# SSD heads, B-by-C and y products: full-height operands and another order of the products

## The chip, the cores and the metric

The kernel runs on one core of a Trainium2 chip, in one launch. The metric is device time in microseconds (us) of that core, the median of several runs. TensorE does the matrix products, VectorE and ScalarE the elementwise work and the emptying of PSUM, GpSimd a few copies and sums; SyncE issues all loads and stores.

## The reference

One layer of a hybrid decoder on 304 token columns: 16 meta tokens, 256 prompt tokens, and 8 running sequences of 4 tokens each. Model width is 2048, everything in fp32.

- `proj = rmsnorm(x) @ w_in`; its columns go to an RG-LRU group and to a Mamba-2 SSD group (z, xs, B, C, dt).
- SSD: 32 heads of 64 features in 4 groups; each group has one B and one C of 128 states. The tokens go in chunks of 128. With `acum` the running sum of `dt*A` inside a chunk:

```
lmat   = exp(acum_i - acum_j) * dt_j          (j <= i, per head)
y_diag = ((C_i . B_j) * lmat) @ xs_j          (inside a chunk)
states = sum_j B_j xs_j exp(acum_end - acum_j) dt_j ;  h = decay * h + states
y_off  = (C_i . h_start) * exp(acum_i)        (from the chunks before)
y      = y_diag + y_off + d_skip * xs ;  then gated by silu(z), normed, projected
```

- After it `x + mix @ w_out`, an MLP `relu(x @ w_up)^2 @ w_down`, and a last norm. The states of both groups are outputs too.

## The kernel before

Everything is kept with features on the partitions and the 288 or 304 tokens along the free axis. Each dense layer is a row of blocks: a block takes 16 k-slices of a 2048x128 piece of weights. The weights arrive in fp32 (1 MB a block, `prep`, L78) and are split into a high part (`whi`, ScalarE) and a low part (`wlo`, VectorE), so that a block is 48 products in fp32r (`gemm`, L101: high by high, high by low, low by high). A block uses two halves of 8 slices; `whi` and `wlo` have four buffers each, which is two blocks.

The SSD work has no stretch of its own. It is a generator, `ssd_core(g)`, one for each of the 4 groups, and `pump()` advances it by one step after every fourth k-slice of a block. So the SSD products lie between the products of the xs and z blocks, from about 143 to 366 us. The program's order is a proposal: the framework's planner, which simulates a timeline (`schedule_with_timeline_sim=True`), puts each engine's instructions in order by readiness and priority, and engines then run in that order.

What matters in `tables` and `ssd_core`:

- `acst` (tables) holds `acum` in two parts: rows 0 to 31 the high part of the 32 heads, rows 32 to 63 the low part. `selr` is a matrix of zeros and ones that picks a head's two rows. Both have 64 rows. The columns of `acum` itself come from weights tiled four times, so its rows 64 to 127 hold copies.
- `head(j)`, for 8 heads a group: one product (L500) of `selr`'s column, broadcast to 128 output rows, with `acst` (288 columns), which puts a head's `acum` on all 128 partitions; then five ScalarE operations read that bank.
- B by C (L471 to L473): two 128x128x128 products in plain fp32 for the prompt chunks, and one for the 32 running tokens, with 32 columns of B as weights, written to 32 partitions. `bd` is a tile with four copies of B's running tokens' 32 columns, made on GpSimd, which L460 has transposed just before.
- `tile_y(t)`, for 4 tiles of 128 features a group: for each chunk c two products of 64 weight columns (L559: one for each head of the tile, written to partitions 0 to 63 and 64 to 127), then one of 128 weight columns (L561, C by the state). `em[c]` is the weighted decay, made by one ScalarE and one VectorE operation a chunk.
- `sample(b)` (L436, L438) treats one running sequence, 8 times a group; its states come and go by DMA.

A plain fp32 product appears in the trace as two records; an fp32r one as one record.

Of the kernel before, what the change touches and what calls it, by code (L numbers as in the profile page):

```python
# [9 lines left out]
F32R = mybir.dt.float32r  # L10
AF = mybir.ActivationFunctionType
# [3 lines left out]
P = 128  # L15
T = 304
M0 = 16
NT = 288
# [11 lines left out]
K_ID, K_MASK, K_SCAN, K_MS, K_ES, K_MB, K_SEL = 0, 128, 256, 560, 592, 720, 728  # L30
# [3 lines left out]
def body(ctx, tc, I, O):  # L34
    nc = tc.nc
    V, A, G, TE, SY = nc.vector, nc.scalar, nc.gpsimd, nc.tensor, nc.sync
# [10 lines left out]
    def nm(s):  # L47
        cnt[0] += 1
        return f"{s}_{cnt[0]}"

    def bigt():
        return big.tile([P, T], F32, tag="big", name=nm("big"))

    def bank():
        return pss.tile([P, 512], F32, tag="s", name=nm("s"))

    def tt(e, out, a, b, op):
        e.tensor_tensor(out, a, b, op=op)  # L58

    def stt(out, a, s, b, op0, op1):  # L60
        V.scalar_tensor_tensor(out, a, s, b, op0=op0, op1=op1)

    def act(out, in_, f, bias=None, scale=None):
        kw = {}
        if bias is not None:
            kw["bias"] = bias
        if scale is not None:
            kw["scale"] = scale
        A.activation(out, in_, f, **kw)  # L69
# [74 lines left out]
    con = cst.tile([P, NCST], F32, name="con")  # L144
# [39 lines left out]
    sp = spa_stack.enter_context(tc.tile_pool(name="spa", bufs=1))  # L184
# [80 lines left out]
    def softplus(out, xin, tmp):  # L265
        ab, r, s, q, acc = tmp
        act(ab, xin, AF.Abs)
        act(ab, ab, AF.Exp, scale=-1.0)
        V.tensor_scalar(r, ab, 2.0, None, op0=ADD)
        V.reciprocal(r, r)  # L270
        tt(V, s, ab, r, MUL)
        tt(V, q, s, s, MUL)
        V.tensor_scalar(acc, q, 1.0 / 17.0, None, op0=MUL)
        for k in (15, 13, 11, 9, 7, 5, 3):
            stt(acc, acc, 1.0 / k, q, ADD, MUL)
        stt(acc, acc, 1.0, s, ADD, MUL)
        V.tensor_scalar(r, xin, 0.0, None, op0=MAX)
        stt(out, acc, 2.0, r, MUL, ADD)
# [44 lines left out]
    def flat(t):  # L323
        return t[:].rearrange("p a b -> p (a b)")

    def dup(e, out, src):
        e.tensor_copy(out[:, 0:3, :], src[:, None, 272:T].to_broadcast([out.shape[0], 3, 32]))
        e.tensor_copy(out[:, 3, :], src[:, 0:32])

    def post_dt(ps):  # L330
        x0 = bigt()
        tt(V, x0[:], ps[:, :T], rsb[:], MUL)
        gens.append(tables(x0))

    def tables(x0):
        b1, b2, b3 = [bigt() for _ in range(3)]
        dt = sp.tile([P, EXT], F32, tag="cv", bufs=2, name="dt")[:, :T]
        th1, th2 = [sp.tile([P, EXT], F32, tag="th", bufs=2, name=nm("th"))[:, :T] for _ in range(2)]
        V.tensor_scalar(x0[:], x0[:], par[:, C_DTB:C_DTB + 1], None, op0=ADD)
        softplus(dt, x0[:], (b1[:], th1, th2, b2[:], b3[:]))  # L340
        nega = cst.tile([P, 1], F32, name="nega")
        act(nega[:], par[:, C_AL:C_AL + 1], AF.Exp)
        V.tensor_scalar(nega[:], nega[:], -1.0, None, op0=MUL)
        dta = x0[:]
        V.tensor_scalar(dta, dt, nega[:], None, op0=MUL)
        acum = b1[:]
        V.tensor_tensor_scan(acum, con[:, K_SCAN:K_SCAN + T], dta, 0.0, op0=MUL, op1=ADD)
        acst = sp.tile([64, NT], F32R, tag="acst", name="acst")
        act(acst[:], acum[0:64, M0:T], AF.Copy)
        tt(V, acst[32:64, :], acum[32:64, M0:T], acst[32:64, :].bitcast(F32), SUB)  # L350
        selr = sp.tile([64, 32], F32R, tag="selr", name="selr")
        act(selr[:], con[0:64, K_SEL:K_SEL + 32], AF.Copy)
        t1 = b2
        V.tensor_copy(t1[0:32, :], dt[0:32, :])
        V.tensor_copy(t1[32:64, :], acum[32:64, :])
        t1d = sp.tile([64, 4, 32], F32, name="t1d")
        dup(V, t1d, t1[0:64])
        yield
        pt = bank()
        ptv = pt[:, 0:192].rearrange("p (c j) -> p c j", j=64)  # L360
        for c, src in enumerate((t1[0:64, 16:144], t1[0:64, 144:272], flat(t1d))):
            TE.transpose(ptv[:, c, :], src, con[0:64, K_ID:K_ID + 64])
        tok = sp.tile([P, 3, 64], F32, name="tok")
        V.tensor_copy(tok[:], ptv)
        yield
        yield
        pl = bank()
        plv = pl[:, 0:96].rearrange("p (c j) -> p c j", j=32)
        for c in (0, 1):
            TE.matmul(plv[:, c, :], con[:, K_ID + 127:K_ID + 128].to_broadcast([P, P]), tok[:, c, 32:64],  # L370
                      start=True, stop=True)
        TE.matmul(plv[:, 2, :], con[:, K_ES:K_ES + P], tok[:, 2, 32:64], start=True, stop=True)
        pd = bank()
        pdv = pd[:, 0:256].rearrange("p (b j) -> p b j", j=32)
        for b in range(8):
            TE.matmul(pdv[:, b, :], con[0:32, K_ID + 4 * b + 3:K_ID + 4 * b + 4].to_broadcast([32, P]),
                      tok[0:32, 2, 32:64], start=True, stop=True)
        we = sp.tile([P, 3, 32], F32, name="we")
        tt(V, we[:], plv, tok[:, :, 32:64], SUB)
        act(we[:], we[:], AF.Exp)  # L380
        decp = sp.tile([P, 2, 32], F32, name="decp")
        act(decp[:], plv[:, 0:2, :], AF.Exp)
        eas = sp.tile([64, 32], F32, name="eas")
        act(eas[:], tok[0:64, 2, 32:64], AF.Exp)
        decs = sp.tile([P, 8, 32], F32, name="decs")
        act(decs[:], pdv, AF.Exp)
        tab.update(tok=tok, we=we, decp=decp, eas=eas, decs=decs, acst=acst, selr=selr)
# [10 lines left out]
    def ssd_core(g):  # L398
        hs = slice(8 * g, 8 * g + 8)
        tok, we, decp, eas, decs, acst, selr = (tab[k] for k in ("tok", "we", "decp", "eas", "decs", "acst", "selr"))  # L400
        B, C = bf[g], cf[g]
        bd = sp.tile([P, 4, 32], F32, tag="dup", bufs=1, name=nm("bd"))
# [67 lines left out]
        pc = bank()  # L470
        TE.matmul(pc[:, 0:128], B[:, 16:144], C[:, 16:144], start=True, stop=True)  # L471
        TE.matmul(pc[:, 128:256], B[:, 144:272], C[:, 144:272], start=True, stop=True)
        TE.matmul(pc[0:32, 256:288], B[:, 272:T], C[:, 272:T], start=True, stop=True)  # L473
        cbm = sq_.tile([P, NT], F32, tag="cbm", name=nm("cbm"))
        tt(V, cbm[:, 0:256].rearrange("p (c j) -> p c j", j=128), pc[:, 0:256].rearrange("p (c j) -> p c j", j=128),
           con[:, None, K_MASK:K_MASK + 128].to_broadcast([P, 2, 128]), MUL)
# [20 lines left out]
        def head(j):  # L497
            h = 8 * g + j
            pbc = bank()
            TE.matmul(pbc[:, 0:NT], selr[:, h:h + 1].to_broadcast([64, P]), acst[:], start=True, stop=True)  # L500
            for c in (0, 1):
                act(em[c][:, j, :], pbc[:, 128 * c:128 * c + 128], AF.Relu, bias=tok[:, c, 32 + h:33 + h], scale=-1.0)
            act(es[:, j, :], pbc[0:32, 256:288], AF.Relu, bias=tok[0:32, 2, 32 + h:33 + h], scale=-1.0)
            q = 64 * (j % 2)
            act(ea[q:q + 64, j // 2, :], pbc[q:q + 64, 0:256], AF.Exp)
# [8 lines left out]

        head(0)
        head(1)
        yield
        sample(0)
# [34 lines left out]
        def tile_y(t):  # L553
            o = 4 * g + t
            py = bank()
            for c in (0, 1):
                for q in (0, 1):
                    j = 2 * t + q
                    TE.matmul(py[64 * q:64 * q + 64, 128 * c:128 * c + 128], xdc[c][:, 64 * j:64 * j + 64],  # L559
                              em[c][:, j, :], start=True, stop=True)  # L560
                TE.matmul(py[:, 256 + 128 * c:384 + 128 * c], hst[c][:, 128 * t:128 * t + 128],  # L561
                          C[:, 16 + 128 * c:144 + 128 * c], start=True, stop=True)
            y = bigt()
            yp = y[:, 0:256]
            tt(V, yp, ea[:, t, :], py[:, 256:512], MUL)
            stt(yp, xf[o][:, M0:272], par[:, C_DSK + o:C_DSK + o + 1], yp, MUL, ADD)
            tt(V, yp, yp, py[:, 0:256], ADD)
            ys_.append(y)

        tile_y(0)  # L570
        yield
        sample(5)
# [30 lines left out]
    def post_x(o):  # L603
        def f(ps):
            xf[o] = bigt()
            post_conv(ps, o, xf[o], rsb if o < 4 else None)
            if o % 4 == 3 and o > 3:
                gens.append(ssd_core(o // 4))
        return f
# [19 lines left out]
    cm = sq_.tile([P, 592], F32R, name="cm")  # L629
    V.tensor_scalar(cm[:], con[:, 0:592], 0.0, None, op0=MUL)  # L630
    gens.append(ssd_core(0))
    run_blocks([(win[8 + o], xa, 0, T, post_x(o)) for o in range(4, 16)], win[24:26])

# [426 lines left out]
```

## Time and profile before

| what | value |
|---|---|
| median of 3 runs | 1643.75 us (1643.62 to 1644.5) |
| the profiled execution | 1644.08 us, of which the span from first to last instruction is 1642.2 us |
| mean granted TensorE clock | 0.995 |
| TensorE busy | 1620.9 us, 99% of the span |
| VectorE busy | 1057.7 us, 64% |
| ScalarE busy | 832.5 us, 51% |

Busy times are unions of records. Records of TensorE overlap (the array works on several products in a pipeline), so the duration of a record is not what a product costs; the distance from one record's start to the next one's is. The form of a TensorE record, as 128*128 or 64*128, is rows of weights by columns of weights.

### The profile page before, as it was taken

Reading aid. Unit: us, or ns where it says so; the run is one execution under the profiler, and the core shown is the slowest. Engines: PE = TensorE matmul, PEld = TensorE weight load, DVE = VectorE, ACT = ScalarE, POOL = GpSimd, SP = SyncE. Lnnn points to the kernel's source line nnn. Section 1 sums busy time; section 2 is a strip of 40 time slices with the busy share of each in tenths; the row PEclk is TensorE's granted clock in tenths of the full one; section 3 lists DMA queues with packets and bytes.
Section 4 is the critical chain, followed back from the end, with each engine's and each line's share of the span. In section 5 each row is a group of like instructions: output and inputs, shape, how many; then the busy total and the mean of one; then the engine's idle time right before and its main releaser. Section 6 shows DMA issues by size and latency. Waiting matters only on the chain.

```text
span 1642.2 us, 28891 instructions
## 1 busy us (share of the span) xinstructions
PE 1620.9 (99%) x11855; PEld 1582.3 (96%) x11855; DVE 1057.7 (64%) x1542; ACT 832.5 (51%) x1299; POOL 243.9 (15%) x311
## 2 busy tenths in 40 slices
PE   7999999999999999999999999999999999999997
PEld 6999888889999999999999999999999999999997
DVE  8998998979887778455565433554444555555554
ACT  5656676557777775344444433443334433344442
POOL 5543323321132321001140000000000000000000
PEclk9999999999999999999999999999999999999999
DMA  6454555544545456544444544545444444544442
GB/s 216 157 178 139 193 183 174 172 176 149 185 140 187 140 182 198 175 169 165 158 172 159 166 168 158 176 154 176 158 166 169 158 176 155 175 158 166 169 158 105
DMA packets 53988, 274.28 MB, mean 167 GB/s; under 512 B 5984, under 2 KB 12768, under 8 KB 24544
## 3 DMA queue, kind: packets, MB, share of 16 engines
q1 hardware_dynamic: 53856, 272.44, 48.7%
q8 instruction: 93, 1.52, 0.4%
q14 instruction: 39, 0.32, 0.1%
HBM read 259.99 MB, written 12.42 MB: 166 GB/s over the span
## 4 chain that ended last, share of the span: by engine, by line
PE 98%; DMA 1%; DVE 0%; SPq 0%; issue 0%; ACT 0%; DVEq 0%
PE g L101 90%; PE s L101 1%; PE s L438 1%; PE s L761 1%; PE s L561 1%; PE s L559 1%; PE s L500 1%; PE s L436 0%; PE s L509 0%; DMA wraw<-in_win 0%; PE s L448 0%; DVE z L58 0%; PE s L520 0%; PE s L586 0%; DMA big<-in_x 0%; SPq L209 0%
## 5 line engine op out<-in xcount | busy, mean ns | idle before, releaser
L58 DVE TENSOR_TENSOR wlo<-wraw,whi 128x1024 fp32r<-128x1024 f32 (+1 forms) x470 | 574.8, 1225 | 427.7 <-ACT whi L69 427.1
L69 ACT ACTIVATE whi<-wraw 128x1024 fp32r<-128x1024 f32 (+1 forms) x470 | 492.2, 1048 | 666.3 <-PE g L101 606.8
L101 PE MATMUL g<-mh,whi 128*128 128x288 f32 x1024 | 303.2, 296 | 0.0
L101 PE MATMUL g<-hh,whi 128*128 128x288 f32 x1024 | 303.0, 296 | 0.0
L101 PE MATMUL g<-hl,whi 128*128 128x288 f32 x1024 | 302.4, 295 | 0.0
L101 PE MATMUL g<-ml,whi 128*128 128x288 f32 x1024 | 302.1, 295 | 0.0
L101 PE MATMUL g<-hh,wlo 128*128 128x288 f32 x1024 | 301.3, 294 | 0.0
L101 PE MATMUL g<-mh,wlo 128*128 128x288 f32 x1024 | 301.1, 294 | 0.0
L101 PE MATMUL g<-xh,whi 128*128 128x288 f32 (+1 forms) x960 | 288.9, 301 | 0.4 <-DVE ext L287 0.4
L101 PE MATMUL g<-xl,whi 128*128 128x288 f32 (+1 forms) x960 | 288.1, 300 | 0.0
L101 PE MATMUL g<-xh,wlo 128*128 128x288 f32 (+1 forms) x960 | 287.9, 300 | 0.0
L101 PEld LDWEIGHTS g<-mh,wlo 128*128 128x128 f32 x1024 | 192.9, 188 | 0.0
L101 PEld LDWEIGHTS g<-hh,wlo 128*128 128x128 f32 x1024 | 192.8, 188 | 0.0
L101 PEld LDWEIGHTS g<-hh,whi 128*128 128x128 f32 x1024 | 192.5, 188 | 0.0
L101 PEld LDWEIGHTS g<-hl,whi 128*128 128x128 f32 x1024 | 192.5, 188 | 0.0
L101 PEld LDWEIGHTS g<-ml,whi 128*128 128x128 f32 x1024 | 192.3, 188 | 0.0
L101 PEld LDWEIGHTS g<-mh,whi 128*128 128x128 f32 x1024 | 191.9, 187 | 0.0
L101 PEld LDWEIGHTS g<-xh,whi 128*128 128x128 f32 x960 | 180.7, 188 | 4.6 <-issue 1.8
L101 PEld LDWEIGHTS g<-xh,wlo 128*128 128x128 f32 x960 | 181.0, 189 | 3.1 <-issue 0.5
L101 PEld LDWEIGHTS g<-xl,whi 128*128 128x128 f32 x960 | 180.8, 188 | 3.4 <-issue 0.7
L101 PE MATMUL g<-lh,whi 128*128 128x288 f32 x256 | 75.7, 296 | 0.0
L101 PE MATMUL g<-sh,whi 128*128 128x288 f32 x256 | 75.7, 296 | 0.0
(273 smaller groups left out, 2323.1 us busy)
## 6 DMA issues: line engine op xcount, KB each, us to landing
wraw<-in_win SPq DMA_DIRECT2D x69, 1024.0 KB, 5.0
wraw<-in_wup SPq DMA_DIRECT2D x64, 1024.0 KB, 4.9
wraw<-in_wdn SPq DMA_DIRECT2D x64, 1024.0 KB, 4.9
wraw<-in_wout SPq DMA_DIRECT2D x32, 1024.0 KB, 5.0
h<-in_stssd SPq DMA_DIRECT2D x32, 256.0 KB, 3.0
out_sssd<-h SPq DMA_DIRECT2D x32, 256.0 KB, 3.2
wraw<-in_win SPq DMA_DIRECT2D x12, 256.0 KB, 6.5
big<-in_x SPq DMA_DIRECT2D x16, 152.0 KB, 3.7
```

The lines of the kernel that those rows point to most:

```text
L58: e.tensor_tensor(out, a, b, op=op)
L69: A.activation(out, in_, f, **kw)
L101: TE.matmul(o, a[:, k % 8, :], b[:, c0:c1], start=n == 0, stop=n == 3 * NK - 1)
L438: TE.matmul(po[0:66, :], cm[:, 66 * b:66 * b + 66], a[:], start=b == 0 and n == 0, stop=b == 7 and n == 1)
L500: TE.matmul(pbc[:, 0:NT], selr[:, h:h + 1].to_broadcast([64, P]), acst[:], start=True, stop=True)
L559: TE.matmul(py[64 * q:64 * q + 64, 128 * c:128 * c + 128], xdc[c][:, 64 * j:64 * j + 64], em[c][:, j, :], start=True, stop=True)
L561: TE.matmul(py[:, 256 + 128 * c:384 + 128 * c], hst[c][:, 128 * t:128 * t + 128], C[:, 16 + 128 * c:144 + 128 * c], start=True, stop=True)
L761: TE.matmul(pr[:, :FL], w_[:, m, :], x_[:], start=n == 0, stop=n == 2)
```

## The change

Three edits, all in the SSD part.

1. `acst` and `selr` get 128 rows in place of 64. Rows 64 to 127 of `selr` are zeros, so the products have the same value; L500 is called with 128 rows.
2. The B-by-C product for the running tokens takes `bd` flattened (128 columns, four copies of the 32) as weights and writes 128 partitions; only the first 32 are read, as before.
3. In `tile_y` the four L559 products of both chunks are issued first, and then the two L561 products.

```diff
-        acst = sp.tile([64, NT], F32R, tag="acst", name="acst")
-        act(acst[:], acum[0:64, M0:T], AF.Copy)
+        acst = sp.tile([P, NT], F32R, tag="acst", name="acst")
+        act(acst[:], acum[:, M0:T], AF.Copy)
         tt(V, acst[32:64, :], acum[32:64, M0:T], acst[32:64, :].bitcast(F32), SUB)
-        selr = sp.tile([64, 32], F32R, tag="selr", name="selr")
-        act(selr[:], con[0:64, K_SEL:K_SEL + 32], AF.Copy)
+        selr = sp.tile([P, 32], F32R, tag="selr", name="selr")
+        act(selr[:], con[:, K_SEL:K_SEL + 32], AF.Copy)
...
-        TE.matmul(pc[0:32, 256:288], B[:, 272:T], C[:, 272:T], start=True, stop=True)
+        TE.matmul(pc[:, 256:288], flat(bd), C[:, 272:T], start=True, stop=True)
...
-            TE.matmul(pbc[:, 0:NT], selr[:, h:h + 1].to_broadcast([64, P]), acst[:], start=True, stop=True)
+            TE.matmul(pbc[:, 0:NT], selr[:, h:h + 1].to_broadcast([P, P]), acst[:], start=True, stop=True)
...
                     TE.matmul(py[64 * q:64 * q + 64, 128 * c:128 * c + 128], xdc[c][:, 64 * j:64 * j + 64],
                               em[c][:, j, :], start=True, stop=True)
+            for c in (0, 1):
                 TE.matmul(py[:, 256 + 128 * c:384 + 128 * c], hst[c][:, 128 * t:128 * t + 128],
                           C[:, 16 + 128 * c:144 + 128 * c], start=True, stop=True)
```

## Rows read from the trace of the kernel before

**Rows 1.** The page: the span, and the chain that ended last by engine.

```profile
span 1642.2 us, 28891 instructions
...
PE 98%; DMA 1%; DVE 0%; SPq 0%; issue 0%; ACT 0%; DVEq 0%
```

**Rows 2.** The SSD stretch: us, busy us by engine (instructions), clock, DMA.

```profile
143.00:366.00 223.00, 223.00 (x1492) 189.07 (x1492) 195.46 (x324) 140.29 (x316) 76.59 (x92) 0.99 0.51 175
```

**Rows 3.** Waits of TensorE's weight loads, 143 to 366: us, times, longest us.

```profile
PEld s L500 <- issue: 7.4, 26, 0.8
...
PEld s L561 <- issue: 5.5, 32, 0.2
```

**Rows 4.** Timeline of TensorE around a single head: start, us, record.

```profile
150.21 0.30 PE L101 MATMUL g<-xh,wlo 128*128 128x304 f32 x1
150.44 0.40 PE L500 MATMUL s<-acst,selr 64*128 64x288 f32 x1
150.77 0.41 PE L101 MATMUL g<-xh,whi 128*128 128x304 f32 x1
151.01 0.30 PE L101 MATMUL g<-xl,whi 128*128 128x304 f32 x1
151.15 0.30 PE L101 MATMUL g<-xh,wlo 128*128 128x304 f32 x1
```

**Rows 5.** Timeline of TensorE at two heads in a row.

```profile
163.76 0.53 PE L500 MATMUL s<-acst,selr 64*128 64x288 f32 x2
164.22 0.44 PE L438 MATMUL s<-h0h,cm 128*66 128x512 f32 x1
```

**Rows 6.** Timeline of TensorE at the y products, first tiles of group 0.

```profile
184.60 0.48 PE L436 MATMUL s<-xr,bm 128*128 128x512 f32 x1
...
185.53 0.44 PE L559 MATMUL s<-em,xdt 128*64 128x128 f32 x4
...
186.45 0.30 PE L101 MATMUL g<-xh,wlo 128*128 128x304 f32 x1
186.68 0.44 PE L559 MATMUL s<-em,xdt 128*64 128x128 f32 x4
187.05 0.49 PE L561 MATMUL s<-cf,hst 128*128 128x128 f32 x2
187.47 0.44 PE L559 MATMUL s<-em,xdt 128*64 128x128 f32 x4
187.84 0.49 PE L561 MATMUL s<-cf,hst 128*128 128x128 f32 x2
```

**Rows 7.** Timeline of TensorE at B by C, group 1.

```profile
200.94 0.39 PE L471 MATMUL s<-cf,bf 128*128 128x128 f32 x2
201.16 0.39 PE L472 MATMUL s<-cf,bf 128*128 128x128 f32 x2
201.48 0.25 PE L473 MATMUL s<-cf,bf 128*32 128x32 f32 x2
201.66 0.41 PE L101 MATMUL g<-xh,wlo 128*128 128x304 f32 x1
201.90 0.30 PE L101 MATMUL g<-xh,whi 128*128 128x304 f32 x1
```

**Rows 8.** Waits of VectorE, 143 to 366: us, times, longest us.

```profile
DVE h L58 <- PE s L436: 8.4, 10, 2.0
DVE wlo L58 <- ACT whi L69: 6.2, 7, 3.5
```

**Rows 9.** Timeline of VectorE: a low part of weights in the z blocks.

```profile
384.70 1.21 DVE L58 TENSOR_TENSOR wlo<-wraw,whi 128x1024 fp32r<-128x1024 f32 x1
```

**Rows 10.** Timeline of TensorE: the first product that reads it.

```profile
388.69 0.30 PE L101 MATMUL g<-xh,wlo 128*128 128x304 f32 x1
```

**Rows 11.** Groups of instructions of VectorE, 143 to 366: busy us, mean ns.

```profile
L58 DVE TENSOR_TENSOR em<-em,cbm 128x1024 f32<-128x1024 f32 x8 | 10.0, 1284 | 0.4 <-ACT em L69 0.3
```

## The prediction

> **What bounds the kernel now.** I read the page first. The chain that ended last is TensorE for 98% of a span of 1642.2 us [rows 1]; so time is gained where TensorE's own row of products becomes shorter, and nowhere else. The span is one profiled execution of 1644.08 us; 1.9 us lie around it, and it stands 0.3 us above the median of 1643.75, from which I subtract.
>
> Next the windows: the SSD stretch is 223 us long, TensorE is busy in all of it, VectorE in 195.46 (88%), ScalarE in 140.29, and the granted clock is 0.99 [rows 2]. Busy here only means that records overlap without a hole. Whether time is lost has to be read from the distances between starts, so I went to the timeline.
>
> There the reader is to see one thing. As long as the form stays 128 rows by more than 64 columns, a fp32r product of 304 columns starts 0.14 us after the one before (151.01 to 151.15 [rows 4]). Where the form changes, three steps in a row are long. Around a single head they are 0.23 (150.21 to 150.44), 0.33 (to 150.77) and 0.24 us (to 151.01) [rows 4]. The waits of the weight loads put those stops down to nothing that the profile knows: "issue", 26 times for the heads and 32 times at L561, 0.2 us each there [rows 3]. TensorE waits for no other engine at these places; it empties itself, and then the first weights of the new form are loaded in plain view. The 32 are two a tile for 16 tiles: each chunk of each tile goes into the 128*64 form and out again.
>
> **The change part by part.**
>
> *Heads.* 24 of the 32 heads stand alone in the timeline as in rows 4, eight stand in four pairs behind L520 as in rows 5. A single one costs 150.21 to 151.01 = 0.80 us for itself and the products on either side. Without a change of form the neighbours take 0.14 each. The head itself I take at 0.13: that is what the second of a pair costs, 0.46 us for two (163.76 to 164.22 [rows 5]) less 0.33 for one [rows 4]. So 0.80 - 0.41 = 0.39 us a head, and 24 x 0.39 = 9.4 us. Its price cannot be far off at 128 rows: a 304-column product of that form takes 0.14 [rows 4], which would take 0.2 us off the sum. A pair: 0.46 - 2 x 0.13 = 0.20, four times 0.8 us. Entering it is not counted, since L520 before it has 16 rows and keeps its own form.
>
> Here a rule can be set beside the row. The row says 0.39 us for one way in and one way out [rows 4]. The Trainium skill ("TensorE: Matmul & The Clock Gate", section "Single matmul latency") gives about 166 ns at full clock as the part of a lone product that a stream of them hides; taken as an estimate for each of two emptyings it would make the heads 24 x 0.33 = 8.0 us in place of 9.4. I keep 9.4, because the row holds the exposed weight load too.
>
> *B by C.* In group 1 the two records of L472 and L473 and the first product behind take 201.16 to 201.90 = 0.74 us [rows 7]. Afterwards L473 has 128 weight columns, so its two records cost what L471's two do, 200.94 to 201.16 = 0.22 [rows 7], though only 32 columns stream. 0.22 + 0.22 + 0.14 = 0.58, a gain of 0.16, times 4 groups 0.6 us. The lower bound is nothing (if four times the weights eat it). No new wait: `bd` is read by L460 shortly before, and the tile that shares its buffer is made at the end of the group.
>
> *y products.* In tiles 1 to 3 of each group the two chunks stand back to back or nearly so: 187.05 to 187.84 = 0.79 us is one L561 and one run of L559 with both changes of form [rows 6]. The new order drops that and adds, without a change of form, four more L559 records (two pairs of 64 columns) behind the first four and two more L561 records behind the first two. The latter are 0.22 as L471's [rows 7]. The former the trace doesn't show, so bounds: a whole run of four is 187.47 to 187.84 = 0.37 with its way out [rows 6], so two pairs are at most 0.37; less the 0.20 that a head's way out costs (0.33 - 0.13 [rows 4, 5]) they are at least 0.17. I take 0.22, since two pairs load as many weight columns as L471's two records, and near the lower end. Gain 0.79 - 0.22 - 0.22 = 0.35 a tile (0.20 to 0.40), for 12 tiles 4.2 us (2.4 to 4.8).
>
> Tile 0 of a group is another matter. Its second chunk starts 185.53, with L436 and more in between (184.60 [rows 6]): the planner had put other work there, because `em[1]` comes one VectorE product, 1.28 us [rows 11], after `em[0]`. It will very likely do so again and pull L561 ahead. Four tiles at 0 to 0.40; I take half of 0.35, 0.7 us in all.
>
> *The rest at nothing.* The copies for `acst` and `selr` happen once, with as many columns as before. ScalarE has 83 us free in the stretch [rows 2] to cover them; uncovered they could cost some tenths. No DMA is added or moved. VectorE's and ScalarE's work stays the same.
>
> TensorE's row shrinks by 9.4 + 0.8 + 0.6 + 4.2 + 0.7 = 15.7 us; from the bounds 13.2 to 17.2.
>
> *What is late next.* The stretch becomes 223 - 15.7 = 207 us, with 195.46 us of VectorE work in it [rows 2]: 94%. VectorE must therefore close its own waits. The two largest are 8.4 us on L436 and 6.2 us on `whi` [rows 8]; the first is TensorE's doing, the second in part, since `whi` waits for buffers that TensorE frees. If all 14.6 us close, VectorE lags by 15.7 - 14.6 = 1.1 us, less than its reserve where I find it thinnest, in the z blocks: a `wlo` ends at 385.91 [rows 9] and is used at 388.69 [rows 10], 2.8 us later. If only half closes, it lags by 8.4, and 8.4 - 2.8 = 5.6 us are given back. So 0 to 5.6; I take 2.0, nearer to the low end, because waits on a faster engine tend to close and gains come 0.39 us at a time while single waits reach 2.0 us [rows 8].
>
> Net 15.7 - 2.0 = 13.7: 1643.75 - 13.7 = 1630.0 us.
>
> **The rivals.**
>
> *VectorE becomes the bound* and gives back more than 4 us. For: 94% over the stretch. Against: weights are split well ahead inside it. At 5.6 us the time is 1643.75 - 15.7 + 5.6 = 1633.6; to 1638 if 10 are lost.
>
> *The long steps have another cause*, some wait that stays. Then little more than B by C is left, and the time is 1643 to 1644. For: "issue" names no cause. Against: the same step at 32 places of L561, where nothing else is common [rows 3].
>
> *64-row products share the array, and 128 rows lose that.* The Trainium skill ("TensorEngine Tiling", section "Tiling Modes", under "Key Properties") lets tiles work independently, and its "Theoretical Speedup" promises up to twofold for 64 rows. Here two heads in a row would have to cost little more than one; the second costs 0.13 us, as much as its columns need [rows 5]. If the four pairs did lose 0.13 each, 0.5 us: 1630.5.
>
> *Slower: the wait for `em[1]`.* If the planner keeps the written order in tile 0, the third L559 stands at the head of TensorE's queue until `em[1]` is made, and all weight products wait behind it. One VectorE product is 1.28 us [rows 11], four groups 5.1 us, still less than the gain. It decides from 15.7 / 4 = 3.9 us a group, which takes two more VectorE products of that size queued ahead; at 5 us a group the time is 1643.75 - 15.7 + 20 = 1648.
>
> **How the numbers follow.** The forecast has 0.68 (1626.5 to 1633: the 17.2 us bound, and 13.2 less a few given back), VectorE as the bound 0.20, another cause 0.06, shared array 0.02, the wait for `em[1]` 0.04. The range 1625.5 to 1636.5 takes the forecast, the shared array and most of VectorE's case; its upper end is 13.2 - 5.6 = 7.6 us below today, 1636.2. About 0.2% (3.3 us) is what a measurement can tell from no change. Faster by more 0.90, within 0.06, slower 0.04.
>
> **What would show it.** In the profile of the changed kernel L500 has the form 128*128 and its steps to the next product are 0.13 to 0.14 us, with no "issue" wait at it. L559 stands in runs of eight in at least 12 tiles, with about 0.11 us a pair, and the count of waits at L561 falls from 32 to 16 to 20. L473 is 128*128 and takes 0.22. The SSD stretch ends 12 to 16 us sooner, and everything behind keeps its length. I am wrong if TensorE shows new waits on VectorE or ScalarE at L559, L438 or L101 in sum above 4 us, if the z blocks become longer, or if the planner scatters the eight L559.

## The result, and the profile after

| | us |
|---|---|
| before, median | 1643.68 |
| changed kernel, median of 4 runs (1631.34 to 1635.99) | 1633.32, ratio 0.9939 (interval 0.9927 to 0.9951) |
| changed kernel measured again, 4 runs (1631.46 to 1632.72), before 1643.75 | 1631.71, ratio 0.9928 (0.9912 to 0.9945) |
| profiled executions, before and after | 1644.08 and 1631.34 |

The kernel is faster by 10.4 us in one measurement, 12.0 in the other, and 12.7 between the two profiled executions. The forecast was 13.7 us. Both medians lie in the stated range of 1625.5 to 1636.5; the first, 1633.32, lies 0.3 us above the narrower 1626.5 to 1633 of the forecast itself.

The page of the changed kernel, the lines that answer to [rows 1]: the span is 13.0 us shorter, and TensorE's share of the chain that ended last falls from 98% to 92%.

```profile
span 1629.2 us, 28889 instructions
...
PE 92%; DMA 3%; DVE 2%; ACT 1%; issue 1%; POOL 0%; SPq 0%; DVEq 0%; POOLq 0%; ACTq 0%
```

The same 223 us as in [rows 2], of the changed kernel. They now hold work that used to come later (1597 records of TensorE in place of 1492); VectorE's 204.11 us are 92%, and TensorE has 0.9 us without any record.

```profile
143.00:366.00 223.00, 222.10 (x1597) 199.93 (x1597) 204.11 (x347) 147.26 (x328) 89.93 (x97) 1.00 0.55 184
```

Waits of TensorE's weight loads there, against [rows 3]. The nameless stops at the heads fall from 26 to 4. The four that are left, 0.76 us each, stand behind the 16-row product L520, and they were among the 26 before, as long as now. At the second kind of y product (now L562) the stops fall from 32 to 16.

```profile
PEld s L500 <- issue: 3.0, 4, 0.8
...
PEld s L562 <- issue: 2.7, 16, 0.2
```

Timeline of TensorE at a single head, against [rows 4]. The three long steps are gone: 0.14, 0.12, 0.15 us.

```profile
148.31 0.30 PE L101 MATMUL g<-xh,wlo 128*128 128x304 f32 x1
148.45 0.29 PE L500 MATMUL s<-acst,selr 128*128 128x288 f32 x1
148.57 0.31 PE L101 MATMUL g<-xh,whi 128*128 128x304 f32 x1
148.72 0.30 PE L101 MATMUL g<-xl,whi 128*128 128x304 f32 x1
```

A pair of heads, against [rows 5]: 161.35 to 161.72 is 0.37 in place of 0.46. The first of the two heads takes 0.24 us as before, since it still follows L520's other form; the second takes 0.13 in place of 0.22. The product behind takes 0.23 in place of 0.28.

```profile
161.35 0.53 PE L500 MATMUL s<-acst,selr 128*128 128x288 f32 x2
161.72 0.40 PE L438 MATMUL s<-h0h,cm 128*66 128x512 f32 x1
161.95 0.40 PE L438 MATMUL s<-h0l,cm 128*66 128x512 f32 x1
```

The y products of group 0, against [rows 6]: tile 0 stands in two runs of four, at 180.13 and 181.72, with a state's product at 180.50 in between; tile 3 is one run of eight.

```profile
180.13 0.44 PE L559 MATMUL s<-em,xdt 128*64 128x128 f32 x4
180.50 0.50 PE L436 MATMUL s<-xr,bm 128*128 128x512 f32 x1
...
181.72 0.44 PE L559 MATMUL s<-em,xdt 128*64 128x128 f32 x4
...
190.40 0.66 PE L559 MATMUL s<-em,xdt 128*64 128x128 f32 x8
190.99 0.71 PE L562 MATMUL s<-cf,hst 128*128 128x128 f32 x4
191.63 0.46 PE L587 MATMUL s<-xdt,es 32*32 32x64 f32 x5
```

Eight records take 0.59 us (190.40 to 190.99) where four took 0.37 [rows 6], so the four added ones cost 0.22. From its first record to the next form the tile takes 1.23 us. Before, the same tile took 193.96 to 195.53 = 1.57:

```profile
193.96 0.44 PE L559 MATMUL s<-em,xdt 128*64 128x128 f32 x4
...
195.53 0.63 PE L586 MATMUL s<-xdt,es 32*32 32x64 f32 x8
```

B by C in group 1, against [rows 7]. L473 has left L472 and stands 10 us later, behind the transpose of the same `bd`.

```profile
196.84 0.39 PE L472 MATMUL s<-cf,bf 128*128 128x128 f32 x2
196.98 0.39 PE L101 MATMUL g<-xh,whi 128*128 128x304 f32 x1
197.21 0.30 PE L101 MATMUL g<-xl,whi 128*128 128x304 f32 x1
...
206.66 0.27 PE L460 MATMUL s<-con,bd 128*128 128x128 f32 x1
206.77 0.31 PE L473 MATMUL s<-cf,bd 128*128 128x32 f32 x2
206.91 0.39 PE L101 MATMUL g<-xl,whi 128*128 128x304 f32 x1
207.13 0.30 PE L101 MATMUL g<-xh,wlo 128*128 128x304 f32 x1
```

L472 with the product behind it takes 0.37 (before, with L473 between, 0.74), L460 with its followers 206.66 to 207.13 = 0.47 (before 212.41 to 212.67 = 0.26): together 0.84 against 1.00. The lines before:

```profile
212.41 0.27 PE L460 MATMUL s<-con,bd 128*128 128x128 f32 x1
...
212.67 0.30 PE L101 MATMUL g<-xh,whi 128*128 128x304 f32 x1
```

What is new are TensorE's waits on other engines between 143 and 400 us, where the kernel before has none on this list:

```profile
PE s L762 <- ACT xch L69: 0.7, 1, 0.7
PE s L594 <- ACT yo L69: 0.6, 1, 0.6
PE s L438 <- ACT h0h L69: 0.3, 1, 0.3
```

Read from one start to the next, each costs more than its idle time. At the second of them 305.01 to 305.92 is 0.91 us where 0.13 is usual:

```profile
305.01 0.29 PE L101 MATMUL g<-xh,whi 128*128 128x288 f32 x1
305.92 0.47 PE L594 MATMUL s<-con,yo 96*128 96x96 f32 x3 [0.61 <-ACT yo L69]
```

Read so, the three cost 0.90, 0.78 and 0.42, in sum 2.1 us. The last products of the SSD part (L586, now L587) stand 11.3 us sooner, 354.22 in place of 365.52, a little less than the 12 to 16 us of the prediction's sign.

### The profile page after: what moved, and what is told of

It reads as the page before. It is cut to its first block, busy times and chain, and to the rows that moved or that the text cites. A ratio compares the mean times of both kernels' runs of the same rounds, so it can differ in the third digit from the quotient of the medians.

```text
span 1629.2 us, 28889 instructions
## 1 busy us (share of the span) xinstructions
PE 1606.7 (99%) x11855; PEld 1579.8 (97%) x11855; DVE 1058.2 (65%) x1542; ACT 831.3 (51%) x1299; POOL 254.1 (16%) x311
## 4 chain that ended last, share of the span: by engine, by line
PE 92%; DMA 3%; DVE 2%; ACT 1%; issue 1%; POOL 0%; SPq 0%; DVEq 0%; POOLq 0%; ACTq 0%
PE g L101 86%; DMA out_sssd<-h 1%; PE s L101 1%; PE s L762 1%; DMA wraw<-in_win 1%; PE s L438 1%; DMA h<-in_stssd 1%; ACT whi L69 0%; POOL h0l L58 0%; DVE z L58 0%; PE s L562 0%; DVE h L58 0%; PE s L436 0%; PE s L559 0%; PE s L448 0%
```

## The experiments

Theory: what a change of form costs on TensorE is what the change saves, part by part, and what is given back is given back by VectorE, which is nearly full. Rivals: the long steps have another cause; what is given back comes from elsewhere. Each set of runs has its own runs of the kernel before; their medians lie between 1643.5 and 1643.8.

**The three parts alone, and the whole once more.** `heads_only` has the lines of `acst`, `selr` and L500 of the diff, `y_only` the loop in `tile_y`, `bc_only` the B-by-C line; `after_again` is the changed kernel. The edit of `y_only`, against the kernel before, is one line:

```diff
+            for c in (0, 1):
```

> Edit 1 alone: the heads with 128 rows. If the changes of form are what was paid for, 24 single heads give back 0.39 us each and four pairs 0.15 to 0.2 us each: TensorE's row is 10.0 us shorter, the profiled time about 1634 us, and L559 still stands in 32 runs of four. If the long steps had another cause, L500's neighbours keep steps of 0.23, 0.33 and 0.24 us and the time stays within 2 us of before. If VectorE gives back what TensorE saves only once the saving is large, this part alone loses less than 0.5 us to waits.

Measured 1636.42 (1635.12 to 1637.59), 7.3 us less. The stops at L500 are down to 4 and L559 stands in 32 runs of four. TensorE waits for `bd` and for a state's high part:

```profile
PE s L460 <- POOL bd L328: 1.2, 1, 1.2
PE s L438 <- ACT h0h L69: 0.6, 1, 0.6
```

From start to start these two cost 1.4 us (207.91 to 209.46) and 0.8 us (243.14 to 244.07). So of the 10.0 us expected of TensorE's row 7.3 are seen and 2.2 are given back in waits, with this part alone, where less than 0.5 was expected; 0.5 us stays without a place.

> Edit 3 alone: the order of the y products. If the changes of form are paid for, 12 tiles lose one way in and out each, 0.53 us, and pay 0.22 us for the four products that are left: 0.31 to 0.35 us a tile, 3.8 to 4.2 us in all, a time of about 1639.7 us. Tile 0 of each group stays split in two and gives nothing. If what counts is VectorE, which makes em and takes the products away, the time stays within 1 us of before, since its work is the same.

Measured 1640.92 (1638.79 to 1642.80), 2.8 us less; 12 runs of eight and 8 of four, as expected. The time saved is less than the 3.8 to 4.2 us expected; its profile has waits of 0.8 us at L594, 0.4 at L448 and 0.2 at L460, about what is missing.

> Edit 2 alone: 128 columns of weights for the running tokens' B by C. If the form is what is paid for, four places become 0.15 to 0.25 us shorter, 0.6 to 1.0 us in all, which the times can hardly show; the steps in the timeline show it: L472 to L473 0.22 in place of 0.32 us, and the product behind without its extra 0.1. If four times the weights cost four times the load, L473 itself grows from 0.18 to 0.22 us or more and eats a part of that.

Measured 1643.19 (1642.34 to 1644.39), ratio 0.9997 (0.9988 to 1.0007): not told from no change by time. In its timeline L473 is 211.00 to 211.14 = 0.14 us and the product behind takes 0.23 in place of 0.14, so its price is 0.23 with what it does to its neighbour. Its profile has full clock over the SSD part and no wait of TensorE on another engine from 130 to 1600 us.

> The changed kernel once more, for a second profile beside the three parts on one chip. Both theories expect 1631 to 1636 us. If its runs scatter because the granted clock dips to half in some executions and not in others, then the executions with the lower mean clock are the longer ones, about 1.6 us for each 0.001 of the clock; if waits on other engines scatter, time and clock do not go together.

Measured 1631.71. The parts give 7.3 + 2.8 + 0.6 = 10.7 us, the whole 10.4 in the first measurement and 12.0 in this one. So no loss is seen by joining them, as there would be if a full engine gave back the more the larger the saving is. Times and clocks don't go together: 1631.47 and 1631.46 at 0.995 and 0.996, 1632.72 at 0.998.

**96 rows.** The heads' operands cut to 96 rows in place of 128.

```diff
-        acst = sp.tile([P, NT], F32R, tag="acst", name="acst")
+        acst = sp.tile([96, NT], F32R, tag="acst", name="acst")
```

> The changed kernel with 96 rows in place of 128 for the heads' two operands. If what was paid for is the array being set to 64 rows and back, 96 rows do as well as 128: L500's next step 0.13 us, no stop of the weight loads at it, the time 1631 to 1635 us. If the number of rows itself counts, or the sharing of the array by small products, the steps around L500 become long again, up to 0.39 us a head, and the time goes up towards 1641 us.

Measured 1631.72 in one run; no stop is named at L500 but the four behind L520. So the price did not come from having fewer than 128 rows: products of 96 rows stand between those of 128 without a stop, products of 64 rows did not. How the 0.39 us of a 64-row head divide between the emptying of the array and the load of the next weights, no run separates.

**Less work for VectorE.** The kernel leaves out the `d_skip` term of the prompt tokens and the last tap of the convolution for the x columns (`taps` is 3 there).

```diff
-            stt(yp, xf[o][:, M0:272], par[:, C_DSK + o:C_DSK + o + 1], yp, MUL, ADD)
...
-        for k in range(1, 4):
+        for k in range(1, taps):
```

> The changed kernel without some 17 us of VectorE's work in and around the SSD stretch: left out are the d_skip term of the prompt tokens (16 operations of 0.55 us) and the last tap of the convolution of the x columns (16 of 0.5 to 0.66 us in the convolutions that precede the SSD work of their group). If TensorE's new waits of some 2.5 us go back to VectorE being nearly full, they go away: 1629 to 1630 us. If they come from ScalarE's queue, GpSimd or the states' loads and stores, they stay or move: 1631 to 1634 us.

Measured 1634.78 (1634.44 to 1636.67), 1.5 and 3.1 us above the two medians of the changed kernel, though the first of these has a run of 1635.99. From 143 to 366 us VectorE is busy 192.28 us, 12 less than in the changed kernel, and TensorE's waits are

```profile
PE s L438 <- ACT h0h L69: 3.2, 4, 1.2
PE s L438 <- POOL h0l L58: 0.5, 2, 0.3
```

This speaks against the theory of VectorE: with room on VectorE, TensorE waits longer, for the states of the running sequences. It does not rule it out, since the planner orders all engines anew for this kernel.

**Without most of the stores of states.** The kernel leaves out 28 of the 32 stores.

```diff
-            SY.dma_start(O["sssd"][g, :, b, :], h0[:])
+            if b == 0:
+                SY.dma_start(O["sssd"][g, :, b, :], h0[:])
```

> The changed kernel without seven of every eight stores of the running sequences' new states (28 of 32 are left out; only the first sequence of a group is stored). A state's buffer is then free when VectorE has added to it, not when its store has landed, and the next load starts earlier. If TensorE's new waits of the changed kernel (at L438 on the high part h0h or the low part h0l of a state, 0.4 to 1.1 us in each profile) come from the chain store, load, split of a state, they go away and the time is 1629.5 to 1631. If they come from VectorE or ScalarE being full, they stay, and the time is 1631 to 1633.

Measured 1631.42 (1630.43 to 1633.27), not told from the changed kernel. The waits at L438 are gone, as the chain of store, load and split demands, and those at L594 and L762 with them; in their place stands

```profile
PE s L461 <- POOL bd L328: 1.2, 1, 1.2
```

**Five buffers for the states.**

```diff
-                h0 = sq_.tile([P, 512], F32, tag="h0", bufs=4, name=nm("h0"))
+                h0 = sq_.tile([P, 512], F32, tag="h0", bufs=5, name=nm("h0"))
```

> The changed kernel with five buffers for the states in place of four (the space is taken from two of the 24 buffers of the pool called big). Nothing is left out. If the load that waits for the store just before it is what holds up L438, the load now finds a free buffer, the waits at h0h and h0l fall below 0.3 us in sum, and the time is 1629.5 to 1631.5. If the two missing buffers of the other pool are needed, or the waits have another cause, the time is 1631.5 or more.

Measured 1632.79 (1631.49 to 1634.31). The wait at L438 is 0.3 us, and small ones on VectorE add up to 1.2 (L559, L436); no gain. What the two buffers taken from `big` cost was not measured by itself.

**Further places of the same kind.** `em_joint` makes both chunks' decay at once; `best3` adds L520 and L376 at 128 rows; `h5_meta` has these two with five state buffers and separate decays; `meta_dup2` has them with two buffers for `bd`. Of the cuts below the first is that of `em_joint` and `best3`, the second that of `best3`, `h5_meta` and `meta_dup2`, the third that of `meta_dup2`; the rows of L376 and the zeros in L520's weights are not shown.

```diff
-            act(em[c][:], em[c][:], AF.Exp, scale=-1.0)
+        act(em2[:], em2[:], AF.Exp, scale=-1.0)
...
-        TE.matmul(ph[:], bt[96:112, 2, :], xw[96:112, :], start=True, stop=True)
+        TE.matmul(ph[:], bt[:, 2, :], xw[:], start=True, stop=True)
...
-        bd = sp.tile([P, 4, 32], F32, tag="dup", bufs=1, name=nm("bd"))
+        bd = sp.tile([P, 4, 32], F32, tag="dup", bufs=2, name=nm("bd"))
```

> The changed kernel with the weighted decay of both chunks made in one ScalarE and one VectorE operation, so that both chunks of tile 0 are ready at once. The planner then has all eight L559 records of each tile in one run, 16 runs in place of 20. By the price of a way in and out (0.09 before, 0.15 inside the run, 0.10 behind) this gives back four times 0.34 us, 1.4 us: 1630 to 1631 us. If readiness of em was not what split tile 0, or if waiting for the joint product costs more than it saves, the time is not below that of the changed kernel.

Measured 1641.62, scattered from 1634.46 to 1648.03. The 16 runs of eight are there, but TensorE waits more:

```profile
PE s L594 <- ACT yo L69: 2.3, 2, 1.4
PE s L559 <- DVE h L58: 0.7, 2, 0.6
```

That the one long ScalarE operation (1.9 us a group) makes others late is not shown. In front of the first of the two waits at L594 ScalarE itself stood 1.8 us until a state's load had landed, and made `yo` right behind it. The profile is one of the shorter runs; the long ones were not profiled.

> The joint decay, and the same idea in two more places: the product of 16 rows at the start of each group (L520, four times, with 0.09 us in, 1.05 for itself and 0.10 behind) takes 128 rows, with the other rows of its weights set to zero by one more ScalarE operation a group, and the eight products of 32 rows in the tables (L376, once) take 128 rows of the identity and of tok. By the row of L509, which has the same shape with 128 rows (0.46 us), L520 gives 0.78 us a group, 3.1 us; L376 some 0.3; with the joint decay 4.8 us: about 1627 us. If TensorE is no longer what bounds the stretch, because VectorE or the states' loads and stores set the pace, half or less of this is seen: 1629 us or more.

Measured 1639.10 (1631.51 to 1643.58). The profiled execution is the shortest of them and has waits of 1.4 us on VectorE, 1.3 on `h0l` and 0.7 on `h0h`; what the longer ones wait for wasn't profiled.

> The same five buffers, and L520 and L376 with 128 rows as before (3.1 and 0.3 us of TensorE's own row), but with em made in two halves again. If the states' chain was what gave back the gain of the last kernel, the 3.4 us are now seen: 1626.5 to 1628.5, with runs that agree within 2 us. If the gain is given back all the same (VectorE full, joint em innocent), 1631 or more with scattered runs.

Measured 1631.05 (1630.67 to 1632.27), ratio 0.9926 (0.9914 to 0.9938), the lowest median here, though its interval covers the changed kernel's second ratio of 0.9928. My price for L520 was misread. In this kernel the timeline shows

```profile
160.57 1.02 PE L521 MATMUL s<-xw,bt 128*128 128x512 f32 x2
161.03 0.82 PE L501 MATMUL s<-acst,selr 128*128 128x288 f32 x2
161.69 0.39 PE L438 MATMUL s<-h0h,cm 128*66 128x512 f32 x1
```

The two records stand 0.46 us before the next start, but the pair of heads behind them then takes 0.66, where 0.13 a head is usual: part of the long plain fp32 product is paid at its follower. From L520 (L521 here) to L438 it is 1.12 us in place of 1.42 in the changed kernel (160.30 to 161.72). With 0.1 less at the product in front, that is a gain of 0.4 a group, not 0.78. Against these 1.6 us and some 0.3 at L376 stand waits of 1.5 us (`bd` 1.0, `h0h` 0.5).

> The changed kernel with L520 and L376 at 128 rows (3.4 us of TensorE's own row by the rows of L509 and L376), four state buffers as in the changed kernel, and two buffers in place of one for the tile bd shares with the sums at a group's end (one of the 24 buffers of big pays for it), so that GpSimd can make bd early: the wait of L460 on bd was 1.3 us in the last profile. If waits can be taken away one by one, the time is 1628 to 1629.5 us, below the changed kernel. If the stretch is so full that a wait taken away turns up somewhere else, at h0h, h0l or yo, it is 1630.5 to 1632.5, no better than the changed kernel.

Measured 1633.39 (1631.64 to 1634.45). The second buffer did not take the wait for `bd` away, and the waits for the states are longer than in the changed kernel:

```profile
PE s L438 <- ACT h0h L69: 2.1, 2, 1.8
PE s L438 <- POOL h0l L58: 2.0, 1, 2.0
PE s L460 <- POOL bd L328: 1.2, 1, 1.2
```

## Why the prediction was right, and where its steps were not

*The cause of the long steps* was right. 24 single heads are worth 0.39 us each (0.80 before, 0.41 in the timeline after), and 96 rows do as well. The rivals of another cause, of shared rows and of a wait for `em[1]` in front of everything are out: the stops went with the form, the pairs of heads became shorter and not longer, and the planner kept tile 0 in two.

*The sum on TensorE's row* was 15.7 and is about 14.7: heads 9.4 as reckoned; pairs 4 x 0.14 = 0.6, not 0.8, since the first head behind L520 still takes 0.24 us and not the 0.13 I had put; B by C 4 x 0.16 = 0.6 as reckoned; y products 12 x 0.34 = 4.1 against 4.2; tile 0 nothing where I had put 0.7. That half chance was the largest error of the sum. The lower bound of 13.2 us was also added up wrongly: with B by C at its own lower bound of nothing it is 12.6, and the slowest end of VectorE's case 1636.8 in place of 1636.2.

*"No new wait" for B by C* was wrong in its reason, and so is "just before" in the description of the kernel: L460 transposes `bd` 11 us after L472 in group 1 (212.41 against 201.16). The planner moved L473 behind it, and no wait at L473 is on the list of the changed kernel.

*What is late next* was the step that failed in its cause, though not in its size. I had VectorE, with 0 to 5.6 us, and took 2.0; the three named waits cost 2.1. That the size fits is luck: the waits stand elsewhere, on ScalarE's copies `yo` and `xch` and on the split of a state, and in the repeat of the same kernel only the two at L438, with 0.4 us each, are named. For `yo` the chain goes back to the states' loads and not to VectorE. ScalarE stood 1.85 us until a state had landed, split it, and made `yo` only then:

```profile
304.62 0.63 ACT L69 ACTIVATE h0h<-h 128x512 fp32r<-128x512 f32 x1 [1.85 <-DMA h<-in_stssd]
305.28 0.59 ACT L69 ACTIVATE yo<-s 32x512 f32<-32x512 f32 x1
```

In front of `xch` it was busy without a break, 1.28 us of it loading a table:

```profile
393.42 1.28 ACT L69 ACT_TABLE_LOAD   x1
...
395.12 0.47 ACT L69 ACTIVATE xch<-xc 128x328 fp32r<-128x328 f32 x1
```

The prediction counted ScalarE only by its 83 free us in the stretch; the row shows that a copy is late all the same where it stands behind another that waits for a load. The reserve of VectorE in the z blocks did shrink as argued:

```profile
376.50 1.22 DVE L58 TENSOR_TENSOR wlo<-wraw,whi 128x1024 fp32r<-128x1024 f32 x1
```

```profile
377.78 0.41 PE L101 MATMUL g<-xh,wlo 128*128 128x304 f32 x1
378.02 0.30 PE L101 MATMUL g<-xh,whi 128*128 128x304 f32 x1
```

That low part ends at 377.72 and is used at 377.78, against 2.8 us of reserve in [rows 9, 10], but it costs only 0.1 us. "Everything behind keeps its length" fails by the 0.9 us at L762, the first LRU product.

*The clock* was not in the sum. Here is the profile before at 146.0 to 149.4: half clock (granted 0.51), 16 TensorE records, where the changed kernel has 28 at full clock. Ahead of it TensorE ran the tables' small products without a stop, among them L376's sixteen records of 32 columns from 142.78 to 144.68, as it did in the changed kernel, where the clock did not fall.

```profile
146.00:149.40 3.40, 3.40 (x16) 3.14 (x14) 3.30 (x8) 0.10 (x1) 2.08 (x6) 0.51 0.00 0
```

`y_only`, which differs from before only in products from 180 us on, has full clock there, and from L362 to L520 takes 136.12 to 162.13 = 26.01 us; before, 135.11 to 162.71 = 27.60. The old forms are not the reason: `em_joint`, which has all three edits, has half clock at the same place (0.50 from 146.2 to 149.6). So 1.6 us of the 13.0 between the two profiles come from the clock of one execution, and without them the profiles differ by 11.4, between the two medians' 10.4 and 12.0. The balance of the spans is then 14.7 - 2.1 + 1.6 = 14.2 against 13.0 measured; 0.2 us of the rest is a later start (the tables' product L362, 138.56 in place of 138.33), and 1.0 us I can't assign.

*Open* stays why the first four runs of the changed kernel reach to 1635.99 and the second four only to 1632.72: one execution of each set was profiled, and none of the long ones. That the waits differ from one execution to the next is shown by the changed kernel and its repeat: `xch`, `yo` and `h0h` in the first, `h0l` and `h0h` in the second. The start differs too: the product L362 of the tables starts at 138.56 us in the first and at 139.49 in the repeat, and likewise at 138.33 in the kernel before and at 139.34 in `y_only`, which has no edit ahead of it. That these two make the long runs long is argued, not shown.

## What to carry to other kernels

Look at the steps between starts wherever the form of a product changes: here a single product with 64 rows among full ones cost 0.39 us more than itself, and one more run of products with 64 weight columns 0.34 us. Rows of zeros or another order took that away without more work on another engine, but for one copy of 128 rows in place of 64. Look also for what the engines behind stand waiting for, and not only for the one that is busiest: here the waits that came up stood at the states' loads and at ScalarE, and each further saving of 1 to 3 us, or each wait removed, showed no gain clear of the scatter, with waits at other places. And price a plain fp32 product together with its follower, since 0.4 us of the one measured here stood there.

## What the runs showed of the hardware

Half clock can stand behind a wait of TensorE, but it need not. In `meta_dup2` 2.14 us passed from a start at 340.96 to the next at 343.10, and then TensorE ran at half clock, in steps of 0.24 in place of 0.13 us. In the same execution 2.27 us from 236.24 to 238.51 were followed by full clock, and the half clock of the kernel before at 146.0 came with no wait at all.

```profile
343.10 0.69 PE L438 MATMUL s<-h0h,cm 128*66 128x512 f32 x1 [1.85 <-ACT h0h L69]
343.10:346.50 3.40, 3.40 (x13) 3.30 (x14) 2.57 (x7) 0.00 (x0) 1.28 (x1) 0.50 0.76 241
...
238.51 0.44 PE L438 MATMUL s<-h0l,cm 128*66 128x512 f32 x1 [1.98 <-POOL h0l L58]
238.50:242.00 3.50, 3.49 (x28) 2.69 (x28) 3.50 (x5) 0.37 (x1) 1.19 (x1) 1.00 0.78 227
```

And with 128 weight columns a plain fp32 product cost no less for streaming fewer columns. L473 with 32 columns takes 0.14 us (206.77 to 206.91) and 0.08 more at its follower (206.91 to 207.13 = 0.22 in place of 0.14). L472 with 128 columns takes the same 0.14 (196.84 to 196.98) and 0.09 more at its follower.
